# Hybrid encoder block on one core: a fourth input projection joins the three that run side by side, and the row factors' transpose moves behind the emptied accumulators

## The chip, the core and the metric

The kernel runs on one core of a Trainium2 chip. The metric is the device time of one execution in microseconds (us); the profile gives the span of one execution, from its first to its last instruction, and the same execution's own time stands beside it below. The engines are TensorE (PE, with its weight loads shown as PEld), VectorE (DVE), ScalarE (ACT), GpSimd (POOL) and SyncE (SP, which here issues most of the transfers).

## The reference

One layer over 256 tokens of width 2048, in float32. What matters here is the front of it:

```python
u = rms_norm(h, norm_mix_w)                 # h = x, 256 x 2048
z = u @ w_in                                # 2048 x 11264, split:
hq, hf, hi, hg, aq, ak, av, gates = ...     # hq, hf, hi, hg: 1024 columns each
f = sigmoid(hf);  g = lb + (1 - lb) * f;  log_g = log(g);  kk = 1 - g
q = silu(hq) * 128 ** -0.5
o = hgrn2_scan(q, kk, hi, log_g)            # 8 heads of 128, chunks of 64
...                                         # chunked attention, gates, w_out, MLP, final norm
```

`rms_norm` divides each token by the root of its mean square. The kernel applies the weight `norm_mix_w` to x before the product and the division (one factor for each token) after it.

## The kernel before

Everything is computed with matmuls on pairs of numbers: a float32 operand is split into a high part (a copy rounded to the fast float32 form) and a low part (the rest), and three partial products are summed. For each weight tile, ACT makes the high part `wh` (L91) and DVE the low part `wl` (L92) from the loaded `raw`. There are six buffers for `raw` and four each for `wh` and `wl`; a buffer holds four k tiles of a projection that is 256 columns wide (or two k tiles of one 512 wide).

The hq and hf projections are computed transposed, 256 columns (two heads) at a time, into two PSUM banks: the weight tile is loaded into the array and the activations stream through it (`mm_t`, L183 for the high parts with 512 columns, L188 for the low ones with 256). One k tile of one such projection is four matmuls; it is called a unit below. There are 16 k tiles. Afterwards `add_parts` sums the two halves of each bank into SBUF: ACT copies one half (L196), DVE adds the other (L197).

The kernel begins with three projections side by side: hf0, hq0 and hf1 (the first 256 columns of hf and hq, and the second 256 of hf). A loop walks over the k tiles (one, one, then two at a time): it loads x transposed (`xw`, L286), makes the high and low part of the activations (`act_x`; for the first two k tiles both on DVE, L294 and L297, then ACT L296 and DVE L297), and issues the units of each projection for these k tiles. Transfers are issued by SP in the order of the program: x, hf0, hq0, hf1, x, hf0, ..., two k tiles (256 KB) each. For the k tiles 1 and 2, `tc.issue_after` puts DVE's work on the activations behind the last low part of the k tile before.

There are eight PSUM banks in three pools: `ps_acc` with four (hf0 and hq0 here, later nearly all accumulators), `ps_tp` with two (transposes) and `ps_sm` with two (hf1 here; small products later).

Behind the loop stand, in the program's order: `add_parts` of f0 and z0; the sums of squares of x (`squares`, L277) and from them `rstd`, the factor of each token; `rows(rstd)`, which widens the factors on DVE (L309), transposes them on PE with two matmuls (L312) into a bank of `ps_tp`, and copies them to SBUF on DVE (L314), so that each row holds all 256 factors; `add_parts` of f1; and the fourth projection, hq1, alone (`gemm_t`, loads of 512 KB), with its `add_parts`. Then come the hi projection (`v_chunk`, L141 to L143, untransposed, 512 columns) and hg.

What is done with f and z (`hf_pair` and `hq_pair`, L392 to L417) needs the rows of factors, and feeds the factors of the HGRN2 scores (L497 to L545, DVE and ACT), which are spread behind the k tiles of hi and hg by a queue of later steps (`later`, `tick`). The first of the score matmuls (L455) stands at the end of that queue, in the hg projection; it uses the banks of `ps_sm` and `ps_tp`.

The order of each engine's instructions is made before the run by a scheduler: it takes, by priority, what its own model of time holds to be ready. The priority is the program's order; blocks of `tc.high_priority` (the splits, `add_parts`) go ahead. On the chip each engine then runs its list.

Of the kernel before, what the change touches and what calls it, by code (L numbers as in the profile page):

```python
# [8 lines left out]
F32 = mybir.dt.float32  # L9
# [3 lines left out]
ALU = mybir.AluOpType  # L13
# [3 lines left out]
P = 128  # L17
T = 256
NM = T // P
D = 2048  # L20
KD = D // P
FF = 8192
NC = 512
# [9 lines left out]
C_HQ, C_HF, C_AQ, C_AK, C_GA, C_GB = 0, HG, 2 * HG, 3 * HG, 4 * HG, 4 * HG + D  # L33
# [3 lines left out]
def bc(ap, pos, n):  # L37

    dims = [list(d) for d in ap.ap]
    dims.insert(pos, [0, n])  # L40
    return bass.AP(tensor=ap.tensor, offset=ap.offset, ap=dims)
# [9 lines left out]
def tile_hybrid_block(  # L51
# [5 lines left out]
    nc = tc.nc  # L57
# [8 lines left out]
    ps_acc, ps_tp, ps_sm = [cm.__enter__() for cm in ps_cms]  # L66
# [23 lines left out]
    def split(hi, lo, src, copy=None):  # L90
        casts[:] = [(copy or nc.scalar.copy)(hi, src)]  # L91
        low[:] = [nc.vector.tensor_tensor(lo, src, hi.bitcast(F32), op=ALU.subtract)]  # L92
        return low[0]

    def rsqrt(dst, ssq, n, width, ms=None):

        if ms is None:
            ms = small.tile([P, width], F32, name="ms", tag=f"ms{width}")
        nc.vector.tensor_scalar(ms, ssq, 1.0 / n, EPS, op0=ALU.mult, op1=ALU.add)  # L99
        nc.gpsimd.tensor_tensor(dst, ms, mhalf[:, :width], op=ALU.pow)  # L100

    def new_act(what):

        return apool.tile([P, 4, 2, T], F32R, name=f"act_{what}", tag="act")
# [8 lines left out]
    def weights(w, n0, nkt, ncols, what, pieces=None, kt0=0, first=False):  # L113

        kpr = 4 * NC // ncols
        half = kpr // 2
        pieces = list(pieces or ())
        for k0 in range(0, nkt, half):
            raw, wh, wl = (wpool.tile([P, 2 * NC], d, name=f"{t}_{what}_{k0}", tag=t, bufs=n).rearrange("p (a n) -> p a n", n=ncols)
                           for t, d, n in (("raw", F32, 6), ("wh", F32R, 4), ("wl", F32R, 4)))  # L120
            k8 = (kt0 + k0) % kpr
            a = 0
            while a < half:
                n = pieces.pop(0) if pieces else half
                if n > 1 or not a % 2:
                    two = max(n, 2)
                    nc.sync.dma_start(raw[:, a:a + two, :], w[n0 // ncols, (kt0 + k0) // kpr, :, k8 + a:k8 + a + two, :])
                with tc.high_priority(offset=2000):
                    split(wh[:, a:a + n], wl[:, a:a + n], raw[:, a:a + n], nc.vector.tensor_copy if n == 1 and first else None)
                for j in range(a, a + n):  # L130
                    yield k0 + j, wh[:, j, :], wl[:, j, :]
                a += n

    def new_bank(what):
        return ps_acc.tile([P, NC], F32, name=f"acc_{what}", tag="acc")

    def new_acc(what):
        return [new_bank(f"{what}{j}") for j in range(2)]
# [11 lines left out]
    def tick(n):  # L150

        if behind:
            behind[0][0] -= n
            while behind and behind[0][0] <= 0:
                behind.pop(0)[1]()
# [13 lines left out]
    def gemm_t(rhs, w, n0, nkt, what, acc=None):  # L169

        acc = acc or new_acc(what)
        for a in weights(w, n0, nkt, T, what):
            tick(1)
            mm_t(acc, rhs, nkt, *a)
        return acc

    def mm_t(acc, rhs, nkt, kt, wh, wl):
        r = rhs[kt // 4][:, kt % 4]
        last = kt == nkt - 1

        def high():
            for cb in range(2):
                newest[:] = [nc.tensor.matmul(acc[cb], wh[:, cb * P:(cb + 1) * P], r.rearrange("p u t -> p (u t)"),  # L183
                                              start=kt == 0, stop=last)]

        def low():
            for cb in range(2):
                newest[:] = [nc.tensor.matmul(acc[cb][:, 0:T], wl[:, cb * P:(cb + 1) * P], r[:, 0, :], start=False, stop=False)]  # L188

        for f in (low, high) if last else (high, low):  # L190
            f()

    def add_parts(dst, acc):
        with tc.high_priority(offset=2000):
            for cb in range(2):
                nc.scalar.copy(dst[:, cb, :], acc[cb][:, T:])  # L196
                nc.vector.tensor_tensor(dst[:, cb, :], acc[cb][:, 0:T], dst[:, cb, :], op=ALU.add)  # L197


    homes = {"extra": False}  # L200
# [44 lines left out]
    def gemm2(lhs, w, n0, nkt, what):  # L245

        acc = [bank(f"{what}{m}") for m in range(NM)]
        for k in range(0, nkt, 2):
            tick(4)
            wh, wl = parts(piece(w, f"{what}{k}", n0, k), f"{what}{k}")  # L250
            for m in range(NM):
                for a in range(2):
                    mm3(acc[m], *lhs_of(lhs, k + a, m), wh[:, a], wl[:, a], k + a == 0, k + a == nkt - 1)
        return acc
# [5 lines left out]
    def h2(what, bufs=10):  # L260
        return hp.tile([P, 2, T], F32, name=what, tag="h2", bufs=bufs)

    xT = [new_act(f"x{c}") for c in range(4)]
    accs = [new_acc("hf0"), new_acc("hq0"), [ps_sm.tile([P, NC], F32, name=f"acc_hf1{j}", tag="sm") for j in range(2)]]
    ws = [weights(w_in_t, C_HF, KD, T, "hf0", (1, 1) + (2,) * 7, first=True),
          weights(w_in_t, C_HQ, KD, T, "hq0", (1, 1) + (2,) * 7),
          weights(w_in_t, C_HF + T, KD, T, "hf1", (1, 1) + (2,) * 7)]
    steps = [1, 1] + [2] * (KD // 2 - 1)
    starts = [sum(steps[:i]) for i in range(len(steps))]

# [5 lines left out]
        nc.sync.dma_start(xr, x[m * P:(m + 1) * P, :])  # L276
        nc.scalar.activation(xr, xr, AF.Square, accum_out=xsq[:, m:m + 1])  # L277

    done = [0, 0, 0]
    for kt, n in zip(starts, steps):  # L280
        c, a = kt // 4, kt % 4
        if kt == 1:
            xw = xw[:, 1:]
        else:
            xw = h2(f"xw{kt}")
            nc.sync.dma_start(xw, x_t[:, kt:kt + 2, :])  # L286
        with ExitStack() as es:
            if kt in (1, 2):
                es.enter_context(tc.issue_after(low[0].ins))
            es.enter_context(tc.high_priority(offset=2000))  # L290
            for j in range(n):
                g, hi = wmix[:, kt + j:kt + j + 1], xT[c][:, a + j, 0, :]
                if kt < 2:
                    nc.vector.tensor_scalar(hi, xw[:, j, :], g, None, op0=ALU.mult)  # L294
                else:
                    nc.scalar.activation(hi, xw[:, j, :], AF.Copy, scale=g)  # L296
                made = nc.vector.scalar_tensor_tensor(xT[c][:, a + j, 1, :], xw[:, j, :], g, hi.bitcast(F32),  # L297
                                                      op0=ALU.mult, op1=ALU.subtract)
        for i in range(3):
            with ExitStack() as es:  # L300
                if kt in (1, 2):
                    es.enter_context(tc.issue_after((low[0] if i else made).ins))
                while done[i] < kt + n:
                    mm_t(accs[i], xT, KD, *next(ws[i]))
                    done[i] += 1
    def rows(factors, what):

        wide = hp.tile([P, NM, P], F32, name=f"wide_{what}", tag="wide", bufs=1)
        nc.vector.tensor_copy(wide, bc(factors, 2, P))  # L309
        tp = ps_tp.tile([P, NM, P], F32, name=f"tp_{what}", tag="tp")  # L310
        for m in range(NM):
            nc.tensor.transpose(tp[:, m, :], wide[:, m, :], ident)  # L312
        r = const.tile([P, T], F32, name=f"rows_{what}")
        nc.vector.tensor_copy(r, tp.rearrange("p m t -> p (m t)"))  # L314
        return r
# [55 lines left out]
    nc.gpsimd.memset(c128, 1.0)  # L371


    f0, z0 = h2("f0"), h2("zq0")
    add_parts(f0, accs[0])
    add_parts(z0, accs[1])
    for m in range(NM):
        squares(m)
    rstd = const.tile([P, NM], F32, name="rstd")
    rsqrt(rstd, xsq, D, NM)  # L380
    rstd_t = rows(rstd, "rstd")
    rstd8 = const.tile([P, T], F32, name="rstd8")[:, 0:NM]
    nc.vector.tensor_scalar(rstd8, rstd, 0.125, None, op0=ALU.mult)

    f1, z1 = h2("f1"), h2("zq1")
    add_parts(f1, accs[2])
    add_parts(z1, gemm_t(xT, w_in_t, C_HQ + T, KD, "hq1"))


    def hf_pair(u, f):  # L390
# [833 lines left out]
    for n in range(2, 4):  # L1224
        for y, w, gate, what in ((ya, w_branch_a, ga[n], "ba"), (yb, w_branch_b, gb[n], "bb")):
            acc = gemm2(y, w, n * NC, 8, f"{what}{n}")
# [222 lines left out]
```

## Time and profile before

| | |
|---|---|
| median of 3 runs | 1363.72 us (1363.05 to 1364.31) |
| profiled execution, its own time | 1363.58 us |
| its span | 1361.9 us |
| PE busy | 1350.3 us (99%) |
| PEld busy | 1116.1 us (82%) |
| DVE busy | 1166.9 us (86%) |
| ACT busy | 970.7 us (71%) |
| chain that ended last | PE 98% |

A row of the timeline reads: start, duration, engine, line, operation, output<-inputs, shape and count, and in brackets how long the engine had been idle before it and what ended that. A row of the stretches gives for each engine the busy time and, in brackets, the count of instructions, then the granted clock of TensorE, the busy share of the DMA engines and the rate of the transfers.

### The profile page before, as it was taken

The numbers are of one execution on the slowest core, as the hardware profiler recorded it, in microseconds if no ns is written. First come the engines' busy times: TensorE is split into PE (matmuls) and PEld (weight loads), VectorE is DVE, ScalarE is ACT, GpSimd is POOL, SyncE is SP. The second block draws the span as 40 slices with busy tenths as digits, with TensorE's granted clock in tenths as the row PEclk, the third lists the DMA queues.
The fourth block names the chain that finished last, engine by engine and source line by source line (L and its number), as shares of the span: only waits on it lengthen the run. The fifth ranks groups of instructions, "written<-read, shape, count | busy, mean of one in ns | idle before, by whom it ended". The sixth has DMA issues, their size and how long they took to land.

```text
span 1361.9 us, 19182 instructions
## 1 busy us (share of the span) xinstructions
PE 1350.3 (99%) x6753; PEld 1116.1 (82%) x6753; DVE 1166.9 (86%) x1406; ACT 970.7 (71%) x1299; POOL 156.3 (11%) x239
## 2 busy tenths in 40 slices
PE   9999999999999999999999999999999999999997
PEld 7888888878778888888888888888888888888886
DVE  6888977887888988798998889898889988899885
ACT  6877765776777666556778767787667876678764
POOL 3000000110110000110121011100121001110210
PEclk9999999999999999999999999999999999999999
DMA  9655557778885988869898889998899988999892
GB/s 347 228 185 157 176 181 264 217 211 258 247 225 171 307 276 246 262 153 325 286 278 264 244 254 263 281 306 225 245 281 275 301 222 238 294 292 274 260 279 97
DMA packets 132498, 336.92 MB, mean 247 GB/s; under 512 B 11296, under 2 KB 14624, under 8 KB 132016
## 3 DMA queue, kind: packets, MB, share of 16 engines
q1 hardware_dynamic: 110816, 266.11, 56.4%
q0 software_dynamic: 21296, 69.28, 26.2%
q8 instruction: 53, 0.87, 0.2%
q14 instruction: 45, 0.37, 0.1%
q10 hardware_dynamic: 288, 0.29, 0.1%
HBM read 271.67 MB, written 10.49 MB: 207 GB/s over the span
## 4 chain that ended last, share of the span: by engine, by line
PE 98%; DMA 1%; ACT 0%; DVE 0%; issue 0%; SPq 0%; POOL 0%; POOLq 0%; DVEq 0%
PE acc_hq L183 2%; PE acc_hf L183 2%; PE tp_u L110 1%; PE acc_hq L188 1%; PE acc_hg L143 1%; PE acc_hi L143 1%; PE acc_hg L141 1%; PE acc_hi L142 1%; PE acc_hg L142 1%; PE acc_ga2c L141 1%; PE acc_hi L141 1%; PE acc_hf L188 1%; PE acc_ga0c L141 1%; PE acc_avc L141 1%; PE acc_dn30c L141 1%; PE acc_wo2c L143 1%
## 5 line engine op out<-in xcount | busy, mean ns | idle before, releaser
L183 PE MATMUL acc_hq<-act_x,wh_hq 128*128 128x512 f32 x128 | 41.0, 399 | 1.5 <-ACT wh_hq L91 1.2
L183 PE MATMUL acc_hf<-act_x,wh_hf 128*128 128x512 f32 x128 | 40.6, 398 | 0.4 <-DVE wh_hf L91 0.4
L1339 POOL DMA_DIRECT2D hd<-y x24 | 24.7, 1041 | 45.8 <-ACT y L1338 45.4
L188 PEld LDWEIGHTS acc_hf<-act_x,wl_hf 128*128 128x128 f32 x128 | 23.4, 188 | 5.4
L188 PEld LDWEIGHTS acc_hq<-act_x,wl_hq 128*128 128x128 f32 x128 | 23.4, 188 | 5.3 <-DVE wl_hq L92 0.2
L141 PE MATMUL acc_hg<-wh_hg,act_x 128*128 128x512 f32 x64 | 25.1, 392 | 0.0
L141 PE MATMUL acc_hi<-wh_hi,act_x 128*128 128x512 f32 x64 | 25.0, 391 | 0.0
L143 PE MATMUL acc_hg<-wh_hg,act_x 128*128 128x512 f32 x64 | 24.9, 390 | 0.0
L143 PE MATMUL acc_hi<-wh_hi,act_x 128*128 128x512 f32 x64 | 24.9, 389 | 0.0
L142 PE MATMUL acc_hi<-wl_hi,act_x 128*128 128x512 f32 x64 | 24.9, 389 | 0.0
L142 PE MATMUL acc_hg<-wl_hg,act_x 128*128 128x512 f32 x64 | 24.9, 389 | 0.0
L92 DVE TENSOR_TENSOR wl_hq<-raw_hq,wh_hq 128x1024 fp32r<-128x1024 f32 (+2 forms) x21 | 20.1, 966 | 5.4 <-ACT wh_hq L91 5.4
L188 PE MATMUL acc_hq<-act_x,wl_hq 128*128 128x256 f32 x128 | 24.6, 279 | 0.0
L188 PE MATMUL acc_hf<-act_x,wl_hf 128*128 128x256 f32 x128 | 24.6, 279 | 0.0
L92 DVE TENSOR_TENSOR wl_hf<-raw_hf,wh_hf 128x512 fp32r<-128x512 f32 (+2 forms) x26 | 20.9, 811 | 4.1 <-ACT wh_hf L91 3.9
L91 ACT CAST wh_hq<-raw_hq 128x1024 fp32r<-128x1024 f32 (+2 forms) x21 | 17.6, 842 | 8.9 <-DMA raw_hq<-in_w_in_t_dram 4.6
L92 DVE TENSOR_TENSOR act_u<-tp_u,act_u 128x512 fp32r<-128x512 f32 x28 | 19.2, 685 | 5.3 <-ACT act_u L91 5.3
L100 POOL TENSOR_TENSOR ro<-os,mhalf 128x4 f32<-128x4 f32 x4 | 4.4, 1099 | 167.4 <-DVE os L99 164.3
L92 DVE TENSOR_TENSOR wl_hg<-raw_hg,wh_hg 128x1024 fp32r<-128x1024 f32 x16 | 19.4, 1219 | 3.0 <-ACT wh_hg L91 3.0
L183 PEld LDWEIGHTS acc_hq<-act_x,wh_hq 128*128 128x128 f32 x128 | 19.9, 189 | 2.2 <-ACT wh_hq L91 1.4
L183 PEld LDWEIGHTS acc_hf<-act_x,wh_hf 128*128 128x128 f32 x128 | 19.9, 190 | 1.0 <-DVE wh_hf L91 0.7
L91 ACT CAST wh_hf<-raw_hf 128x512 fp32r<-128x512 f32 (+2 forms) x24 | 17.5, 740 | 4.4 <-PE acc_hg L143 1.6
(2295 smaller groups left out, 5327.3 us busy)
## 6 DMA issues: line engine op xcount, KB each, us to landing
raw_hi<-in_w_in_n_dram SPq DMA_DIRECT2D x16, 512.0 KB, 3.8
raw_hg<-in_w_in_n_dram SPq DMA_DIRECT2D x16, 512.0 KB, 3.7
raw_hq<-in_w_in_t_dram SPq DMA_DIRECT2D x12, 512.0 KB, 5.2
hd<-y POOLq DMA_DIRECT2D x24, 256.0 KB, 8.6
raw_hf<-in_w_in_t_dram SPq DMA_DIRECT2D x16, 256.0 KB, 5.6
raw_hf<-in_w_in_t_dram SPq DMA_DIRECT2D x8, 512.0 KB, 4.0
raw_aq<-in_w_in_t_dram SPq DMA_DIRECT2D x8, 512.0 KB, 4.4
raw_ak<-in_w_in_t_dram SPq DMA_DIRECT2D x8, 512.0 KB, 4.3
```

Source lines behind the costliest of these rows:

```text
L91: casts[:] = [(copy or nc.scalar.copy)(hi, src)]
L92: low[:] = [nc.vector.tensor_tensor(lo, src, hi.bitcast(F32), op=ALU.subtract)]
L100: nc.gpsimd.tensor_tensor(dst, ms, mhalf[:, :width], op=ALU.pow)
L110: nc.tensor.transpose(tp[:, j, :], src[:, j * P:(j + 1) * P], ident)
L141: nc.tensor.matmul(acc, hi, wh, start=first, stop=False, skip_group_check=True)
L142: nc.tensor.matmul(acc, hi, wl, start=False, stop=False, skip_group_check=True)
L143: newest[:] = [nc.tensor.matmul(acc, lo, wh, start=False, stop=last, skip_group_check=True)]
L183: newest[:] = [nc.tensor.matmul(acc[cb], wh[:, cb * P:(cb + 1) * P], r.rearrange("p u t -> p (u t)"), start=kt == 0, stop=last)]
L188: newest[:] = [nc.tensor.matmul(acc[cb][:, 0:T], wl[:, cb * P:(cb + 1) * P], r[:, 0, :], start=False, stop=False)]
L1339: nc.gpsimd.dma_start(hd[n][m], t, accum_op=ALU.add)
```

## The change

The loop over the k tiles carries four projections instead of three: hq1 joins, with accumulators in the two banks of `ps_tp`, and with loads of two k tiles (256 KB) like the others. It no longer runs alone behind them. All eight banks then hold accumulators. The transpose of the row factors goes to a bank of `ps_sm`, and the instructions that `rows` puts on DVE are ordered behind the last addition of the last `add_parts` (that of z1).

```diff
@@ add_parts
             for cb in range(2):
                 nc.scalar.copy(dst[:, cb, :], acc[cb][:, T:])
-                nc.vector.tensor_tensor(dst[:, cb, :], acc[cb][:, 0:T], dst[:, cb, :], op=ALU.add)
+                added = nc.vector.tensor_tensor(dst[:, cb, :], acc[cb][:, 0:T], dst[:, cb, :], op=ALU.add)
+        return added
@@ ahead of the loop
-    accs = [new_acc("hf0"), new_acc("hq0"), [ps_sm.tile([P, NC], F32, name=f"acc_hf1{j}", tag="sm") for j in range(2)]]
+    accs = [new_acc("hf0"), new_acc("hq0")] + [[pool.tile([P, NC], F32, name=f"acc_{what}{j}", tag=tag) for j in range(2)]
+                                               for what, pool, tag in (("hf1", ps_sm, "sm"), ("hq1", ps_tp, "tp"))]
     ws = [...
-          weights(w_in_t, C_HF + T, KD, T, "hf1", (1, 1) + (2,) * 7)]
+          weights(w_in_t, C_HF + T, KD, T, "hf1", (1, 1) + (2,) * 7),
+          weights(w_in_t, C_HQ + T, KD, T, "hq1", (1, 1) + (2,) * 7)]
@@ the loop
-    done = [0, 0, 0]
+    done = [0] * 4
...
-        for i in range(3):
+        for i in range(4):
@@ rows
-        tp = ps_tp.tile([P, NM, P], F32, name=f"tp_{what}", tag="tp")
+        tp = ps_sm.tile([P, NM, P], F32, name=f"tp_{what}", tag="sm")
@@ behind the loop
-    f0, z0 = h2("f0"), h2("zq0")
-    add_parts(f0, accs[0])
-    add_parts(z0, accs[1])
+    f0, z0, f1, z1 = [h2(what) for what in ("f0", "zq0", "f1", "zq1")]
+    for i, t in enumerate((f0, z0, f1, z1)):
+        added = add_parts(t, accs[i])
     for m in range(NM):
         squares(m)
     rstd = const.tile([P, NM], F32, name="rstd")
     rsqrt(rstd, xsq, D, NM)
-    rstd_t = rows(rstd, "rstd")
+    with tc.issue_after(added.ins):
+        rstd_t = rows(rstd, "rstd")
     rstd8 = const.tile([P, T], F32, name="rstd8")[:, 0:NM]
     nc.vector.tensor_scalar(rstd8, rstd, 0.125, None, op0=ALU.mult)
-
-    f1, z1 = h2("f1"), h2("zq1")
-    add_parts(f1, accs[2])
-    add_parts(z1, gemm_t(xT, w_in_t, C_HQ + T, KD, "hq1"))
```

## The prediction

> **What bounds the kernel now.** I read the page's busy times and its chain of waits first, then the engines' busy time by stretches, then who PE waited for, and last the timeline of the first 55 us.
>
> ```profile
> PE 1350.3 (99%) x6753; PEld 1116.1 (82%) x6753; DVE 1166.9 (86%) x1406; ACT 970.7 (71%) x1299; POOL 156.3 (11%) x239
> PE 98%; DMA 1%; ACT 0%; DVE 0%; issue 0%; SPq 0%; POOL 0%; POOLq 0%; DVEq 0%
> core 0: us, PE busy (x) PEld busy (x) DVE busy (x) ACT busy (x) POOL busy (x), PEclk, DMA share, GB/s
> 0.00:50.00 50.00, 46.98 (x260) 40.79 (x261) 35.91 (x74) 33.73 (x60) 13.92 (x50) 1.00 0.89 323
> 50.00:100.00 50.00, 50.00 (x342) 41.62 (x341) 45.29 (x87) 40.08 (x57) 0.00 (x0) 1.00 0.57 185
> 1350.00:1362.00 12.00, 3.79 (x23) 3.19 (x21) 3.31 (x7) 4.13 (x10) 1.13 (x4) 0.80 0.49 176
> PE acc_hq L183 <- ACT wh_hq L91: 1.2, 1, 1.2
> PE ps_warm L81 <- DVE warm L79: 1.1, 1, 1.1
> PE acc_qkc L141 <- ACT u_qk L872: 0.5, 1, 0.5
> PE acc_hf L183 <- DVE wh_hf L91: 0.4, 1, 0.4
> PE acc_hq L183 <- DVE act_x L297: 0.3, 1, 0.3
> ```
>
> The reader is to see that PE is the bound and that its idle time has few places: 1361.9 - 1350.3 = 11.6 us in all, of which 3.02 lie in the first 50 us, 0.5 in one wait far behind, and about 8.1 in the tail. The last five lines are the whole list of PE's waits. The change takes no matmul away: 16 units of hq1 are issued before and after, and the two transposes too. So it can gain only what it takes from the 3.02 us at the start, and of these the first 1.1 us (until the warm-up matmuls begin) and the 0.4 us for the very first weights stand ahead of anything that it touches. What is left are the waits of 1.17 and 0.33 us, 1.5 in all. That bounds the gain at 0.11%. A loss has no such bound: new waits of PE.
>
> **The start.** These rows of the timeline carry it:
>
> ```profile
> 7.11 0.33 SPq L127 DMA_DIRECT2D raw_hq<-in_w_in_t_dram  x1
> 7.12 0.40 ACT L91 CAST wh_hq<-raw_hq 128x256 fp32r<-128x256 f32 x1 [4.58 <-DMA raw_hq<-in_w_in_t_dram]
> 7.57 0.73 PE L183 MATMUL acc_hq<-act_x,wh_hq 128*128 128x512 f32 x2 [1.17 <-ACT wh_hq L91]
> 7.76 0.33 SPq L127 DMA_DIRECT2D raw_hf<-in_w_in_t_dram  x1
> 7.77 0.41 ACT L91 CAST wh_hf<-raw_hf 128x256 fp32r<-128x256 f32 x1 [0.25 <-DMA raw_hf<-in_w_in_t_dram]
> 8.08 0.40 ACT L91 CAST wh_hq<-raw_hq 128x256 fp32r<-128x256 f32 x1
> 8.21 0.43 DVE L92 TENSOR_TENSOR wl_hf<-raw_hf,wh_hf 128x256 fp32r<-128x256 f32 x1 [0.23 <-ACT wh_hf L91]
> 8.39 0.40 ACT L91 CAST wh_hf<-raw_hf 128x256 fp32r<-128x256 f32 x1
> 8.40 0.33 SPq L286 DMA_DIRECT2D xw<-in_x_t_dram  x1
> 8.55 0.35 DVE L294 TENSOR_SCALAR act_x<-xw,vt 128x256 fp32r<-128x256 f32 x1
> 8.93 0.49 DVE L297 SCALAR_TENSOR_TENSOR act_x<-xw,vt,act_x 128x256 fp32r<-128x256 f32 x1
> 9.57 0.47 PE L183 MATMUL acc_hq<-act_x,wh_hq 128*128 128x512 f32 x1 [0.33 <-DVE act_x L297]
> 20.12 0.62 PE L183 MATMUL acc_hf<-act_x,wh_hf 128*128 128x512 f32 x2
> 20.82 0.63 PE L183 MATMUL acc_hf<-act_x,wh_hf 128*128 128x512 f32 x2
> ```
>
> Two paces are to be seen. SP's issues at 7.11, 7.76 and 8.40 follow landings: the first two stand at the instants at which ACT begins on hq0's and hf1's weights. So 256 KB land every 0.65 us. And a unit on PE takes 20.82 - 20.12 = 0.70 us.
>
> The wait of 1.17 us for hq0's weights stays: they are still the third transfer, all are of 256 KB, and what is put in comes behind them.
>
> The wait of 0.33 us is at the second k tile, whose activations DVE makes behind the last low part of the first. Before, that is hf1's: landed 7.76, ACT's cast 0.41, low part from 8.21, activations 8.55 and 8.93, PE at 9.57; 1.81 us from landing to PE. After, it is hq1's, which lands in the place that x held, at 8.40. With the same 1.81 us PE begins the second k tile at 10.21, which is 0.64 later, while it has done one unit (0.70) more: a gain of 0.06. If ACT first makes the two casts that start at 8.08 and 8.39, hq1's begins at about 8.79, 0.39 later, and the sum is a loss of 0.33. Ends: -0.33 (the wait closes wholly) and +0.33; I take 0, since both orders of ACT are open.
>
> **Side by side, steady.** Four units for each k tile take PE 2.8 us instead of 2.1. For two k tiles the other engines have these durations:
>
> ```profile
> L92 DVE TENSOR_TENSOR wl_hf<-raw_hf,wh_hf x16: 417/680/744, 5.3 to 27.3; 128x512 fp32r<-128x512 f32 x12, 128x256 fp32r<-128x256 f32 x4
> L91 ACT CAST wh_hf<-raw_hf x14: 402/612/622, 7.8 to 26.3; 128x512 fp32r<-128x512 f32 x12, 128x256 fp32r<-128x256 f32 x2
> 38.82 1.05 ACT L91 CAST wh_hq<-raw_hq 128x1024 fp32r<-128x1024 f32 x1
> 40.84 1.22 DVE L92 TENSOR_TENSOR wl_hq<-raw_hq,wh_hq 128x1024 fp32r<-128x1024 f32 x1
> ```
>
> DVE: 4 x 0.68 + 2 x 0.49 = 3.70 us beside 5.6 of PE (before 3.02 beside 4.2, so it has more room). ACT: 4 x 0.61 + 2 x about 0.45 (an estimate from its 0.61 for 512 columns; the activations have 256) = 3.3. The smaller pieces of hq1 cost more in all: ACT 2 x 0.40 + 7 x 0.61 = 5.1 us instead of 4 x 1.05 = 4.2, DVE 2 x 0.43 + 7 x 0.68 = 5.6 instead of 4.9, SP eight issues instead of four at 0.33 each. All of it lies beside PE; cost 0. If DVE's room were gone, the 0.7 would show once.
>
> Two resources get tighter. All four buffers of `wh` and `wl` are now in use at once, so the next cast of a projection waits until PE is through with its last four k tiles. Cast and low part take 0.61 + 0.68 = 1.29 us, and the other three projections' two k tiles give PE 6 x 0.70 = 4.2 us of work meanwhile; cost 0, cover left 2.9. The six `raw` buffers hold four projections and a half: SP stops sooner, and x for the next k tiles is queued behind. But for two k tiles PE takes 5.6 us, and the five transfers land in 5 x 0.65 = 3.25; cost 0.
>
> **The end of the loop.** These rows show it before:
>
> ```profile
> 37.33 0.29 DVE L309 COPY wide_rstd<-rstd 128x256 f32<-128x256 f32 x1 [0.84 <-POOL rstd L100]
> 41.05 0.38 PE L312 MATMUL tp_rstd<-ident,wide_rstd 128*128 128x128 f32 x2
> 46.27 0.42 DVE L314 COPY rows_rstd<-tp_rstd 128x256 f32<-128x256 f32 x1
> 46.72 0.69 DVE L392 TENSOR_TENSOR f<-f,rows_rstd 128x512 f32<-128x512 f32 x1
> 52.41 0.65 ACT L196 COPY zq<-acc_hq 128x256 f32<-128x256 f32 x2 [1.06 <-PE acc_hq L183]
> 52.45 0.39 PE L141 MATMUL acc_hi<-wh_hi,act_x 128*128 128x512 f32 x1
> 52.81 0.76 DVE L197 TENSOR_TENSOR zq<-acc_hq,zq 128x256 f32<-128x256 f32 x2 [0.30 <-ACT zq L196]
> ```
>
> hq1 ends at about 52.4 either way, as PE has the same units to do. hi's first banks are those of hf0, which ends three projections, 4.2 us, earlier; its `add_parts` takes 0.65 + 0.76. hi's first splits need a buffer that hf0 frees at the same time: 1.05 + 1.22 = 2.27 us, or 3.7 behind that `add_parts` in full; still 0.5 us ahead of PE. Cost 0; if that cover goes, some tenths.
>
> The wide copy now waits in DVE's queue behind z1's last addition, which ends at 52.81 + 0.76 = 53.57. Behind it in DVE's queue stand hi's low parts, which have buffers ahead; it waits for nothing else, so they lose its 0.29 alone. The transposes can then begin at 53.9. PE has hi's matmuls to do meanwhile, if the scheduler puts some of them ahead. Then the two transposes cost what they cost before (0.2 to 0.4, paid already): 0. If it puts them directly behind hq1, PE stands from 52.4 to 53.9. Ends 0 and +1.5, with its room for delays +1.9. I take 0, since PE's list of waits has no transposes in it, though the kernel has many whose inputs come from DVE late.
>
> **What comes late.** With the transposes at about 54 and the copy of 0.42 behind them, f times the factors (L392) begins at about 55.5 instead of 46.72, 8.8 us later. Who waits are the score matmuls:
>
> ```profile
> 80.03 0.35 DVE L545 TENSOR_TENSOR ql<-qr,d 128x192 f32<-128x192 f32 x1
> L455 PEld LDWEIGHTS ps_a<-q,kk x128: 106/110/110, 90.6 to 190.6; 128*32 128x32 f32 x128
> 41.00:52.40 11.40, 11.40 (x67) 9.97 (x66) 10.68 (x15) 7.35 (x10) 0.00 (x0) 1.00 0.72 239
> 52.40:76.00 23.60, 23.60 (x105) 19.52 (x104) 22.59 (x39) 22.41 (x30) 0.00 (x0) 1.00 0.57 182
> ```
>
> Their last input (L545) is ready at 80.38, and PE begins them at 90.6: 10.2 us of slack for 8.8 of delay, with 1.4 left even if the chain takes as long as before. It should take less. DVE was busy 10.68 + 22.59 of 35 us from 41 on; of the work on f and z only some 4 us were done before 52.4 (an estimate: the copy of 0.42 and five steps like L392 at 0.69), and hq1's low parts (1.22 each) no longer compete. DVE is idle 50 - 45.29 = 4.7 us between 50 and 100, which takes up these 4. Cost 0; if the cover goes, each us of lateness beyond it is a us of PE.
>
> **The sum**: 0 (start, -0.33 to +0.33) + 0 (steady) + 0 (transposes, to +1.9) + 0 (scores). So the span stays at 1361.9 and the profiled execution at 1363.58, which is 0.14 under the median; in the median's terms I forecast 1363.7 us.
>
> **Rivals.**
> 1. The transposes stand at hi's head, and PE waits for ACT's copy, the addition and the wide copy: 1363.7 + 1.9 = 1365.6. For it: they come first in the program. Against it: at 9.57 PE begins the second k tile with a matmul of hq0, which the program has behind hf0, so its list is made by readiness. What the Trainium skill says in "TensorE: Matmul & The Clock Gate", Part 2 (step by step), speaks for this rival: TensorE pulls weight loads ahead, but matmuls stay in program order, so hi could not pass the transposes. The trace does not disagree: no row shows a matmul passing a waiting one.
> 2. Slower: the work on f and z, 8.8 us late, makes the scores late. It happens if DVE and ACT, in their fixed order, need more than 10.2 us extra; from there every us counts. If the 4.7 us of idle time cannot be used, 8.8 grows to 13.5, and PE waits 3.3: 1367.0. For it: DVE is 22.59/23.60 busy in hi's first half, and ACT 22.41. Against it: the 4.7 us idle, and a list that the scheduler makes for the late data. By the Trainium skill, the same page's Part 1 (the clock gate), a wait of PE of about 3.4 us halves the matmul clock until it has been busy as long again, an estimate of 1.7 us on top. Of this the trace has one hint, the granted clock of 0.80 in the last stretch, where PE is idle 8.1 us, against 1.00 at the start with a gap of 1.17.
> 3. Faster: more work per x closes the 0.33 us, and other orders of ACT close some of the 1.17: 1363.7 - 1.0 = 1362.7. For it: DVE has more room. Against it: nothing in the change brings hq0's weights sooner.
>
> **How the numbers follow.** Forecast 0.70, rival 1 0.13, rival 2 0.09, rival 3 0.08. Within 0.2% (2.7 us, about what a measurement of this kernel can tell from no change) lie the forecast, rival 1 and rival 3, and some of the small cases of rival 2; beyond it, slower, most of rival 2: 0.08; faster than 0.2% is more than the idle time there is to win, 0.02 for what I overlook; the same 0.90. The range: down by 0.33 at the start, 0.5 for the one wait far behind and 0.5 for the runs' own spread, 1362.4; up by 1.9 and the spread, 1366.2. It leaves rival 2 out.
>
> **What would show it.** Right: PE's gap at the second k tile between 0 and 0.7 us; hq1's units in the same stretch as the others, and hi beginning at 52.1 to 52.8; the transposes behind some of hi's matmuls, without a wait; L392 at 54 to 57 and L455 at 90 to 91 with no wait of PE; nothing new in the list of PE's waits. Wrong: a wait of PE at L312 (rival 1), at L141 for hi's low parts (their buffers or DVE's queue), or at L455 and later score matmuls (rival 2); or PE's idle time in the first 12 us under 2.4 us (rival 3).

## The result and the profile after

The changed kernel takes 1371.25 us (median, 1367.51 to 1372.23) where the kernel before takes 1364.14 us on the same chip (1363.05 to 1364.65): a ratio of 1.0047 over the executions, 95% interval 1.0032 to 1.0062 (the two medians alone would give 1.0052). It is slower, by about 7 us. I had forecast 1363.7 us, no measurable change, and a range up to 1366.2. The forecast was wrong, and the range too narrow.

First the same views as of the kernel before: from the page the busy times, then two stretches (granted clock, DMA share and rate stand last), then the whole list of what PE waited for (total us, times, longest us).

```profile
PE 1351.7 (99%) x6753; PEld 1115.8 (82%) x6753; DVE 1167.2 (85%) x1411; ACT 971.1 (71%) x1304; POOL 156.1 (11%) x239
0.00:50.00 50.00, 44.05 (x237) 37.11 (x238) 29.01 (x59) 27.91 (x52) 12.29 (x49) 1.00 0.88 296
50.00:100.00 50.00, 47.53 (x333) 39.50 (x332) 44.49 (x85) 40.11 (x55) 0.72 (x1) 1.00 0.60 199
PE acc_hf L183 <- ACT wh_hf L91: 3.3, 2, 2.7
PE ps_c L479 <- DVE c L537: 2.1, 1, 2.1
PE ps_warm L81 <- DVE warm L79: 1.1, 1, 1.1
PE acc_hf L183 <- DVE wh_hf L91: 0.9, 2, 0.5
PE acc_hq L183 <- ACT wh_hq L91: 0.6, 2, 0.4
PE ps L552 <- DVE ql L545: 0.4, 1, 0.4
PE acc_ga2c L141 <- ACT u_ga L872: 0.2, 1, 0.2
```

The profiled execution took 1369.76 us with a span of 1368.0: 6.1 us more than before. PE does the same matmuls (6753 instructions, 1351.7 us busy against 1350.3). What grew is its idle time: 1368.0 - 1351.7 = 16.3 us against 11.6. The two stretches say where: 5.95 us idle up to 50 us (before 3.02), and 2.47 us between 50 and 100 (before none). New in the list are 2.7 us for a cast of hf's weights, inside the loop, and 2.1 + 0.4 us, in two rows, for factors of the scores.

**The first wait** lies at the end of the loop. These are rows of the changed kernel's timeline: SP's issues, ACT, PE and the first matmul of hi.

```profile
9.61 0.33 SPq L289 DMA_DIRECT2D xw<-in_x_t_dram  x1
10.94 0.74 PE L183 MATMUL acc_hf<-act_x,wh_hf 128*128 128x512 f32 x2 [0.55 <-DVE wh_hf L91]
13.89 0.33 SPq L127 DMA_DIRECT2D raw_hf<-in_w_in_t_dram  x1
34.09 1.62 SPq L279 DMA_DIRECT2D xr<-in_x_dram  x2
38.89 1.14 ACT L91 CAST wh_hq<-raw_hq 128x512 fp32r<-128x512 f32 x2 [0.25 <-PE acc_hq L183]
44.78 1.91 ACT L280 ACTIVATE xr<-xr 128x2048 f32<-128x2048 f32 x1 [4.75 <-DMA xr<-in_x_dram]
46.69 0.60 ACT L91 CAST wh_hf<-raw_hf 128x512 fp32r<-128x512 f32 x1
47.35 0.73 PE L183 MATMUL acc_hf<-act_x,wh_hf 128*128 128x512 f32 x2 [2.69 <-ACT wh_hf L91]
56.12 0.40 PE L141 MATMUL acc_hi<-wh_hi,act_x 128*128 128x512 f32 x1
```

And the kernel before, the same two instructions (its lines stand three lower):

```profile
23.06 0.87 SPq L276 DMA_DIRECT2D xr<-in_x_dram  x2
32.28 1.92 ACT L277 ACTIVATE xr<-xr 128x2048 f32<-128x2048 f32 x1
```

The reader is to see a chain over three queues. SP issues x for the sums of squares (`xr`, two tiles of 1 MB) behind the loop's weights. There is a third more of them, and SP stands still where no `raw` buffer is free (from 9.94 to 13.89, and twice again). So `xr` is issued at 34.09 instead of 23.06. In ACT's list the first sum of squares (L280) stands ahead of the last four casts of the loop. ACT reaches it at 40.0, finds no `xr`, and stands for 4.75 us; the casts of k tiles 14 and 15 stand behind it, and PE waits 2.69 us for the first of them. Before, `xr` was there when ACT came to it at 32.28 (no idle time ahead of that row), and all the casts of the loop stood ahead of the squares. So two things changed together: `xr` comes later, and the scheduler put the square ahead of four casts.

**The second wait** begins with a lateness on DVE and shows on PE 35 us later. DVE and PE of the changed kernel:

```profile
57.10 0.75 DVE L197 TENSOR_TENSOR zq<-acc_hq,zq 128x256 f32<-128x256 f32 x2
57.77 3.62 DVE L92 TENSOR_TENSOR wl_hi<-raw_hi,wh_hi 128x1024 fp32r<-128x1024 f32 x3
61.30 0.29 DVE L312 COPY wide_rstd<-rstd 128x256 f32<-128x256 f32 x1
62.70 0.69 DVE L392 TENSOR_TENSOR f<-f,rows_rstd 128x512 f32<-128x512 f32 x1
97.47 0.28 DVE L526 TENSOR_TENSOR qr<-qr,rr 128x128 f32<-128x128 f32 x1
97.90 0.57 PE L479 MATMUL ps_c<-qr,kl 128*32 128x96 f32 x24 [2.11 <-DVE c L537]
98.83 0.71 PE L552 MATMUL ps<-ql,kc 128*128 128x128 f32 x4 [0.36 <-DVE ql L545]
```

z1's last addition ends at 57.85, but the wide copy starts at 61.30: three low parts of hi stand between them in DVE's list. Measured from the first matmul of hi, L392 comes 62.70 - 56.12 = 6.58 us behind it; before it came 52.45 - 46.72 = 5.73 us ahead. That is 12.3 us later in the pattern. The matmul that waits first, `ps_c`, reads `kl` and `qr`, and the last of these that DVE makes is `qr` (L526; `c`, which the row names, ends just behind it). The kernel before has the same two instructions:

```profile
77.61 0.28 DVE L526 TENSOR_TENSOR qr<-qr,rr 128x128 f32<-128x128 f32 x1
91.67 0.55 PE L479 MATMUL ps_c<-qr,kl 128*32 128x96 f32 x24
```

There `qr` was done 91.67 - 77.89 = 13.8 us ahead of its use; that is the slack. From hi's first matmul to the end of `qr` it takes 97.75 - 56.12 = 41.63 us in the change and 77.89 - 52.45 = 25.44 before. So `qr` comes 16.2 us later in the pattern, and 16.2 - 13.8 = 2.4. The wait is 2.11 + 0.36 = 2.47 us. Of the 16.2 us, 12.3 are there at L392; the other 3.9 are added on the way from L392 to `qr`, which takes 97.75 - 62.70 = 35.1 us instead of 77.89 - 46.72 = 31.2.

How the 6.1 us build up is read from first starts. These are the groups of the first score matmuls and of `po`, the first matmul behind the scores, in the changed kernel, and of `po` in the kernel before (durations, then first and last start):

```profile
L455 PE MATMUL ps_a<-q,kk x128: 206/206/230, 94.6 to 197.3; 128*32 128x48 f32 x128
L580 PE MATMUL po<-v,sd x32: 271/275/275, 130.0 to 208.5; 128*128 128x128 f32 x32
```

```profile
L580 PE MATMUL po<-v,sd x32: 270/275/275, 123.4 to 201.8; 128*128 128x128 f32 x32
```

By these: hi 56.12 against 52.45 (+3.67), the first score matmuls 94.6 against 90.6 (+4.0), and `po` 130.0 against 123.4 (+6.6). Of the 3.67, some 0.7 come from the start: the second k tile begins at 10.94 with four units done, before at 9.57 with three, and a unit takes 0.70. Terms: 0.7 (start) + 3.0 (first wait with what is lost around it) + 0.3 (from hi to the scores, where the two transposes now stand) + 2.6 (scores) = 6.6; some 0.5 of it comes back later (for one, the single late wait in the list is 0.2 us instead of 0.5).

### The profile page after: what moved, and what is told of

It is laid out like the page before. It is cut to its first block, busy times and chain, and to the rows that moved or that the text cites. A ratio compares the mean times of both kernels' runs of the same rounds, so it can differ in the third digit from the quotient of the medians.

```text
span 1368.0 us, 19204 instructions
## 1 busy us (share of the span) xinstructions
PE 1351.7 (99%) x6753; PEld 1115.8 (82%) x6753; DVE 1167.2 (85%) x1411; ACT 971.1 (71%) x1304; POOL 156.1 (11%) x239
## 4 chain that ended last, share of the span: by engine, by line
PE 69%; ACT 0%; POOLq 0%; issue 0%; POOL 0%
PE tp_u L110 1%; PE acc_dn32c L142 1%; PE acc_dn30c L141 1%; PE acc_wo2c L143 1%; PE acc_dn00c L143 1%; PE acc_dn20c L143 1%; PE acc_up00c L143 1%; PE acc_dn20c L141 1%; PE acc_dn32c L143 1%; PE acc_dn00c L141 1%; PE acc_dn32c L141 1%; PE acc_dn10c L141 1%; PE acc_dn30c L143 1%; PE acc_up30c L142 1%; PE acc_up20c L142 1%; PE acc_wo2c L141 1%
## 5 line engine op out<-in xcount | busy, mean ns | idle before, releaser
L92 DVE TENSOR_TENSOR wl_hq<-raw_hq,wh_hq 128x512 fp32r<-128x512 f32 (+2 forms) x26 | 20.8, 811 | 1.8 <-ACT wh_hq L91 1.7
L91 ACT CAST wh_hq<-raw_hq 128x512 fp32r<-128x512 f32 (+2 forms) x26 | 18.1, 715 | 4.7 <-DMA raw_hq<-in_w_in_t_dram 4.4
L91 ACT CAST wh_hi<-raw_hi 128x1024 fp32r<-128x1024 f32 x16 | 17.0, 1060 | 5.7 <-PE acc_hi L143 5.6
```

## The experiments

Theory A: three separate places, the start, the casts behind the late squares, and the scores that DVE's order makes late. Their threshold was taken from the prediction, 10.2 us of lateness at L392; the expectations below still go by it. Its rivals: the late squares cause the scores' wait too; the weights are starved in the whole loop; the side by side form itself costs time. All comparisons below are with the kernel before on the same chip. The unaltered change was run again among them:

> The changed kernel again, unaltered, for a second trace: its five runs lay between 1367.5 and 1372.2. Theory A: PE's wait at the casts follows the landing of x (44.78 in the first trace) one to one; where it comes to be longer than about 3 us, the granted clock falls for a while and the run is longer by more than the wait. If the two waits are the same as in the first trace and the time is not, the spread has another cause.

Measured: 1369.99 us against 1363.22, ratio 1.0049 (1.0036 to 1.0061), with the same waits (2.4 us for the cast, 2.1 for `c`).

**The squares behind the casts.** The changed kernel, in which ACT's squares stand behind the last casts of the loop:

```diff
-    for m in range(NM):
-        squares(m)
+    with tc.issue_after(casts[0].ins):
+        for m in range(NM):
+            squares(m)
```

> The changed kernel with one edit: on ACT the two sums of squares are ordered behind the last cast of the loop. Theory A (two separate waits: PE's 2.69 us at the casts of the last k tiles, which stand in ACT's queue behind a sum of squares whose x lands late; and 2.47 us at the score matmuls, because the row factors reach DVE late): the first wait goes with its restart, some 3 us; the second stays at 2 to 2.5; start 0.2 to 0.7 worse than before. Time about 3 us over the kernel before. Rival B (the four projections starve on transfers and buffers; the square is only where it shows): PE waits elsewhere in the loop, still 6 to 7 over. Rival C (the late squares cause both waits): both go, under 1 us over.

Measured: 1368.72 us, ratio 1.0038 (1.0025 to 1.0050). PE's waits, one stretch and four rows of the timeline:

```profile
PE ps_c L480 <- DVE c L538: 2.1, 1, 2.1
PE acc_hf L183 <- DVE wh_hf L91: 1.5, 2, 0.8
PE acc_hf L183 <- ACT wh_hf L91: 1.4, 1, 1.4
95.00:100.00 5.00, 3.96 (x34) 3.39 (x35) 5.00 (x17) 2.67 (x9) 0.00 (x0) 0.67 0.70 230
91.79 0.39 PE L142 MATMUL acc_hg<-wl_hg,act_x 128*128 128x512 f32 x1
92.02 0.39 PE L143 MATMUL acc_hg<-wh_hg,act_x 128*128 128x512 f32 x1
98.40 0.63 PE L143 MATMUL acc_hg<-wh_hg,act_x 128*128 128x512 f32 x1
98.82 0.63 PE L141 MATMUL acc_hg<-wh_hg,act_x 128*128 128x512 f32 x1
```

The wait of 2.7 us in the loop is gone (the 1.4 left for a cast lies at the start, for hf1's first weights), and hi begins at 53.6 instead of 56.1. `xr` is still late in this run (ACT waits 1.7 us for it), but no cast stands behind it. So the order on ACT, with `xr` late, was the cause of the first wait. The scores' wait stays at 2.1, so the late squares do not cause it; and no wait for weights comes up elsewhere in the loop, so starvation of the loop is excluded as well. But hi came 2.5 us earlier and the time fell by 1369.99 - 1368.72 = 1.3 us only, and the stretch says why: behind the scores' wait the granted clock is 0.67 for 5 us. There the matmuls start 98.82 - 98.40 = 0.42 us apart instead of 92.02 - 91.79 = 0.23. From the first score matmul to `po` it takes 129.4 - 92.3 = 37.1 us here, 35.4 in the changed kernel's profile (granted clock 1.00 in that stretch), and 32.8 before. The slower clock costs 1.7 us in this execution. (`qr` is 16.5 us late here.)

**x for the squares by POOL's queue**, so that it doesn't stand behind the weights in SP's:

```diff
-        nc.sync.dma_start(xr, x[m * P:(m + 1) * P, :])
+        nc.gpsimd.dma_start(xr, x[m * P:(m + 1) * P, :])
```

> The changed kernel with one edit: the two transfers of x for the sums of squares are issued by the POOL queue instead of SP's, where they stand behind the weights that wait for raw buffers. Theory A: x lands before 30 us, ACT does not wait for it, PE's 2.69 us go, the scores' wait of 2 to 2.5 stays, since the rows' copies stand behind four or five of hi's low parts on DVE whenever rstd is ready: about 3 us over the kernel before. Rival B: the 2 MB come into the full stretch of the transfers, weights land later, and PE waits at the start of the loop: 4 to 7 over. Rival C: rstd is ready 14 us sooner, both waits go: under 1 us over.

Measured: 1372.74 us, ratio 1.0071 (1.0058 to 1.0083), no remedy. PE's two longest waits and two stretches, from the longest of its five executions (1375.4 us):

```profile
PE acc_hq L183 <- ACT wh_hq L91: 2.7, 1, 2.7
PE ps_c L479 <- DVE c L537: 2.1, 1, 2.1
20.00:40.00 20.00, 16.69 (x78) 13.67 (x77) 11.21 (x20) 10.30 (x20) 0.00 (x0) 0.83 0.93 315
100.00:105.00 5.00, 3.19 (x32) 2.79 (x33) 5.00 (x16) 2.12 (x7) 0.00 (x0) 0.69 0.66 208
```

`xr` now travels from 13.4 us on, and PE waits 2.7 us for weights that come later by it, between 20 and 40 us, again with a lower clock (0.83 of full over the stretch). The wait at the squares is gone. The scores' wait is the same 2.1 although the squares are done before the loop's end: a second run in which the two waits are separate. Behind it the clock is 0.69 for 5 us, as in the run before.

**The rows late, alone.** The kernel before, hq1 alone behind the loop as ever, with only the row factors' transpose put behind z1's last addition:

```diff
-    rstd_t = rows(rstd, "rstd")
...
+    added = add_parts(z1, gemm_t(xT, w_in_t, C_HQ + T, KD, "hq1"))
+    with tc.issue_after(added.ins):
+        rstd_t = rows(rstd, "rstd")
```

> The kernel before (three side by side, hq1 alone) with one part of the change: the rows of factors are made behind the last addition of z1, still in the transposes' bank. L392's work then begins about 9 us later against hi's start (before 5.7 us ahead of it). Theory A with its threshold (the scores have 10.2 us of slack, each us of lateness beyond is a us of PE): 9 is under 10.2, so no wait at the scores, or some tenths: within 1 us of the kernel before. Rival D (any lateness of several us costs, because DVE and ACT are full there): 2 us or more over, with PE waiting at the score matmuls.

Measured: 1364.4 us against 1363.22, ratio 1.0003 (0.9994 to 1.0013): no change that can be told from none. The row of DVE's timeline:

```profile
54.84 0.69 DVE L394 TENSOR_TENSOR f<-f,rows_rstd 128x512 f32<-128x512 f32 x1
```

This is L392 of the others, with hi at 51.7, 3.2 behind it and so 8.9 us later in the pattern: about the 8.8 that the prediction had reckoned for the change. `qr` is 11.1 us late, under its 13.8 of slack. No score matmul waited.

**The same with more lateness.** As the last, with the wide copy done nine times:

```diff
-        nc.vector.tensor_copy(wide, bc(factors, 2, P))
+        for _ in range(9 if what == "rstd" else 1):
+            nc.vector.tensor_copy(wide, bc(factors, 2, P))
```

> The kernel before with the row factors' transpose behind z1's last add, as in the run that moved the rows alone, and with the copy to wide_rstd done nine times instead of once (eight copies of 0.29 us more on DVE, which also let two of hi's low parts pass): the first use of the rows comes some 4 us later than there, a lateness of about 13 us against the slack of 10.2 us. Theory A: ps_c waits 2 to 2.8 us for c and the time is 1366.8 (1365.8 to 1368.5, the upper part if the granted clock falls behind the wait). If the slack is larger than 10.2 us or DVE makes the lateness good: no wait of ps_c and the time of the kernel before.

Measured: 1368.05 us, ratio 1.0032 (1.0019 to 1.0044). Its timeline and a stretch:

```profile
60.43 0.68 DVE L395 TENSOR_TENSOR f<-f,rows_rstd 128x512 f32<-128x512 f32 x1
94.33 0.57 PE L482 MATMUL ps_c<-qr,kl 128*32 128x96 f32 x24 [2.04 <-DVE qr L529]
95.45 1.20 PE L555 MATMUL ps<-ql,kc 128*128 128x128 f32 x4 [0.55 <-DVE ql L548]
95.00:100.00 5.00, 4.55 (x15) 3.86 (x16) 5.00 (x15) 2.94 (x9) 0.00 (x0) 0.66 0.62 198
```

Hi begins at 52.4, so L395 (L392 in the others) stands 8.1 behind it, 13.8 us later in the pattern. The wait appears, 2.04 + 0.55 us, with nothing else of the change in the kernel (the first of the two rows names `qr` itself as what ended it), and the clock falls behind it to 0.66: `po` is at 128.2 instead of 123.4. By the prediction's 10.2 us the wait should have been 13.8 - 10.2 = 3.6 us, and it is 2.6. Measured at the scores' input it fits: `qr` is 16.5 us late, and 16.5 - 13.8 = 2.7.

**The rows early again.** The changed kernel, in which the row factors' steps and pair 0's first steps on f and z take priority over hi's low parts; the squares stay where the change has them:

```diff
-    with tc.issue_after(added.ins):
+    with tc.issue_after(added.ins), tc.high_priority(offset=4000):
         rstd_t = rows(rstd, "rstd")
...
-    a0[1]()
-    a0[2]()
+    with tc.high_priority(offset=4000):
+        a0[1]()
+        a0[2]()
```

> The changed kernel with the higher priority for the row factors' transpose and pair 0's first steps alone; the squares stay where the change has them. Theory A: the wait of 2.7 us for the casts of k tiles 14 and 15 stays and hi starts near 56.1; ps_c waits under 0.5 us; from ps_a on the lead of the kernel before stays at about 4 us, not 6.5: 1367.6 (1366.5 to 1368.8). If the scores' wait were an effect of the late loop and not of DVE's order, it would stay near 2 us and the time at 1370.

Measured: 1367.74 us, ratio 1.0031 (1.0019 to 1.0043). PE's longest entry, and L392:

```profile
PE acc_hf L183 <- ACT wh_hf L91: 3.4, 2, 1.8
61.49 0.69 DVE L392 TENSOR_TENSOR f<-f,rows_rstd 128x512 f32<-128x512 f32 x1
```

The scores no longer wait: hi is at 57.0, L392 4.5 behind it, 10.2 later in the pattern, and `qr` is 10.1 late: on the way from L392 nothing is added. From the first score matmul to `po` it takes 128.2 - 95.5 = 32.7 us, as before. Of the 3.4 us in two waits, the loop's was 1.6 here, smaller than expected. The start was later (1.8 us of wait for hf1's first cast, and a granted clock of 0.66 from 10 to 15 us), so that PE came to the loop's wait at 46.7 instead of 44.7. The end of that wait is set by `xr`, which came only 0.9 later, so about half of the late start is absorbed in it. The two do not add in full.

**Both together**: the squares behind the casts and the rows early again, in one kernel.

> The changed kernel with two edits in the order alone: the squares behind the last casts of the loop, and a higher priority for the row factors' transpose and for pair 0's first steps on DVE. Theory A (two waits of PE and a later start): L183 waits for no cast at 44 to 48, ps_c waits for c under 0.5 us, hi starts near 53.6 (as with the squares alone behind the casts), ps_a, po and acc_aq follow 1 to 2 us behind the kernel before, and the time is 1365.0 (1364.0 to 1366.0), some 6 us below the changed kernel. Rival D (the side by side form itself costs time, by its banks or its order of matmuls): the two waits go and the time stays at 1368 or above. Rival G (the granted clock falls for a reason other than these waits): the waits go, the clock stays at 0.997 and the time is 1367 to 1368.

Measured: 1364.33 us against 1363.69, ratio 1.0009 (1.0000 to 1.0018). The whole list of PE's waits, from the fastest of its eleven executions (1363.6 us):

```profile
PE acc_hf L183 <- DVE wh_hf L91: 1.3, 2, 0.8
PE ps_warm L81 <- DVE warm L79: 1.1, 1, 1.1
PE acc_hf L183 <- ACT wh_hf L91: 0.7, 1, 0.7
PE acc_hq L183 <- ACT wh_hq L91: 0.4, 1, 0.4
PE tp_u L110 <- DVE act_u L92: 0.3, 1, 0.3
```

With the two waits out of the list, all but 0.6 us of the median is back; in this profile hi begins 0.7 us later than before, and the second k tile 0.9, which points to the start. The span of the profiled execution is 1361.9, that of the kernel before. So the side by side form, its banks and its order of matmuls cost no more than these tenths. They also gain nothing.

**And the start.** Both remedies, and the split of x for k tile 1 put behind the third unit's low part instead of the fourth's (for k tiles 1 and 2, with a higher priority):

```diff
-                es.enter_context(tc.issue_after(low[0].ins))
-            es.enter_context(tc.high_priority(offset=2000))
+                es.enter_context(tc.issue_after(third[0].ins))
+            es.enter_context(tc.high_priority(offset=6000 if kt in (1, 2) else 2000))
...
+            if i == 2:
+                third[:] = [low[0]]
```

> Both waits removed as in the first kernel of this call, and the split of x for k tile 1 behind the third unit's low part instead of the fourth's, so that it is DVE's work ahead of hq1's low part. Theory A: the second k tile starts up to 0.4 us earlier and the time is 1364.6 (1363.6 to 1365.6): no less than the kernel before, as side by side removes no work from PE. If the fourth projection beside the others gains time once its waits are gone: under 1362.5.

Measured: 1365.18 us, ratio 1.0010 (1.0001 to 1.0018): no better. A row of the start and a stretch:

```profile
6.18 0.74 PE L183 MATMUL acc_hf<-act_x,wh_hf 128*128 128x512 f32 x2 [1.67 <-DVE wh_hf L91]
0.00:20.00 20.00, 16.46 (x73) 13.96 (x74) 11.43 (x27) 9.27 (x20) 12.00 (x49) 0.83 0.82 254
```

In this execution the first weights came late (1.67 us of wait), and the clock was lower in the first 20 us. Whether the 0.4 us that the edit moves was gained cannot be read under that. No run pointed to a version that beats the kernel before, as all remedies only give back what the change costs.

## Why the prediction was wrong

The lateness of the first use of the rows (L392) and that of `qr`, the last input of `ps_c`, each counted from hi's first matmul and against the kernel before, beside the scores' wait and the time from the first score matmul to `po`, each from one profile. `qr` has 13.8 us of slack.

| kernel | L392 late, us | `qr` late, us | PE's wait at the scores, us | scores to `po`, us |
|---|---|---|---|---|
| before | 0 | 0 | 0 | 32.8 |
| rows late, alone | 8.9 | 11.1 | 0 | 32.8 |
| rows early again | 10.2 | 10.1 | 0 | 32.7 |
| both remedies | 10.2 | 10.1 | 0 | 32.7 |
| the change | 12.3 | 16.2 | 2.5 | 35.4 |
| squares behind the casts | 12.6 | 16.5 | 2.5 | 37.1 (clock 0.67 behind the wait) |
| x by POOL's queue | 12.3 | 16.2 | 2.4 | 36.8 (clock 0.69 behind the wait) |
| rows late, nine copies | 13.8 | 16.5 | 2.6 | 37.1 (clock 0.66 behind the wait) |

- **The bound of the gain** (1.5 us at the start, a loss without bound) was right in kind: no run beat the kernel before.
- **The start** was put at 0, between -0.33 and +0.33. It cost +0.7 in the changed kernel's profile. The step that failed is the pace of the landings: hf1's and hq1's casts left gaps of 0.66 and 0.19 us ahead of the second k tile's 0.55, where the working had PE busy through the fourth unit. The 1.17 us for hq0's weights, which were to stay, were 0.37. Mis-sized, and small; in other profiles of the same start the second k tile came up to 1.7 us late.
- **"Side by side, steady", cost 0**: this step failed, and it is the first 3.0 us. It says that SP stops sooner at the six `raw` buffers and that "x for the next k tiles is queued behind". I looked at the loop's own x, which came in time, and did not go on along SP's queue to the next thing in it, `xr`, nor ask what would stand behind the sum of squares in ACT's list. The squares were moved ahead of four casts by the change without a line of theirs being touched. The run with the squares behind the casts shows this cause. The covers that I did price (`wh` and `wl` buffers, DVE's and ACT's time) held: no wait shows them.
- **"The end of the loop"** was right as to PE: the transposes stand among hi's matmuls and PE waits for none (rival 1 falls). It failed on DVE. The wide copy was to lose nothing, with hi's low parts behind it in DVE's queue. It stood behind three of them, 3.45 us from z1's addition to the copy, as the splits have the higher priority.
- **"What comes late"** carried the right mechanism, and both terms of its sum failed. The lateness at L392 was reckoned 8.8 and measured 12.3. Of the work from there to the scores it says "It should take less"; it took 3.9 us longer, so that `qr` was 16.2 late. The 10.2 us of slack were read between L545 and the first score matmul, which does not read L545's result. At `ps_c`, which waited, the slack was 13.8. So neither failure was enough alone: 12.3 us with the work as long as before, or 8.8 + 3.9 = 12.7, would have stayed under 13.8. In the table the waits follow from `qr`'s lateness less 13.8 us to within 0.3 us; how lateness at L392 becomes lateness at `qr` differs from kernel to kernel, and no rule for it is shown. The mechanism is rival 2's, which I gave 0.09 and left out of the range. That its price of 3.3 us and its 1367.0 came near the scores' part is partly luck: it is the difference of 13.5 us of lateness and 10.2 of slack, where 16.2 and 13.8 were measured. The spare 4.7 us of DVE, which I set against it, made nothing good in the change.
- **The clock.** Rival 2's sentence on the Trainium skill gave an estimate of 1.7 us on top for a lower clock behind such a wait. The squares-behind-casts run has 37.1 us from the scores to `po` where the change has 35.4: 1.7 us, with the clock at 0.67. By the Trainium skill, "TensorE: Matmul & The Clock Gate", Part 1 (the clock gate), some 3.4 us of idle time halve the clock. The same part of the Trainium skill says of a kernel's start that the count of slow matmuls varies from run to run, as the window in which activity is counted runs freely. Here the measurement decides on the length: 2.1 + 0.4 us of idle time were enough in three profiles, and the same waits in the two profiles of the unaltered change were followed by a full clock.

In medians, each against the kernel before on the same chip, the rows early again are 1367.74 - 1363.69 = 4.1 us over, the squares behind the casts 1368.72 - 1363.22 = 5.5 and both together 0.6. So the first wait's part is 3.4 us and the scores' part 4.9, the latter with the lower clock. With 0.6 for the rest they make 8.9, more than the 6.8 to 7.1 of the change. The two profiles with one remedy each have a slower clock in them somewhere, and the two profiles of the change have none. But that does not close the sum: the mean granted clock that was recorded with each execution is 0.996 or 0.997 in six of the change's ten and in two of 38 of the kernel before, so the change has executions with a slower clock too, of which no timeline is on record. Why the clock fell behind this wait in some kernels' profiles and not in others' stays open, and with it the last 2 us of the sum.

## What to carry to other kernels

When a loop takes more loads, follow each queue past the loop to the next thing in it, then go to the engine that consumes that thing and read what stands behind the consumer in its list: a late transfer stops everything behind it there, even work whose inputs are ready. When a producer is ordered "behind the last addition", list what the scheduler will put between them (here the splits with a higher priority), add what the work from there to the consumer will take in its new place, and hold the sum against the slack at the instruction that reads the result. If the two lie within a few us of each other, give the late case a real chance and let the range reach it. A form that takes no work from the bounding engine can gain no more than its idle time, while each new wait costs in full.

## What the runs showed of the hardware

A wait of PE of 2.1 us was followed in three profiles by a granted clock of 0.66, 0.67 and 0.69 over 5 us; in the first two, matmuls started 0.42 us apart instead of 0.23 for 3 to 4 us. From the scores to `po` these three profiles took 1.4 to 1.7 us longer than the change's, more than half of what the wait itself cost. In the changed kernel's two profiles the same wait had no such sequel. I had not expected so short a wait to be enough, nor the difference between the profiles.
